# Three spacer tiles on the right side of SBUF: other byte offsets between the two operands of the matmuls

## The chip, the cores and the metric

The kernel runs on one core of a Trainium2 chip. The metric is the device time of one execution in microseconds (us). Before the change it is 840.83 us, the median of three runs (839.64 to 841.19).

## What is computed

The reference is one layer of a bidirectional encoder: 512 positions, 1024 features, float32, batch 1. In its order, with the sizes that matter:

```python
n = rms_norm(x, norm_mix_pre)                     # 512 x 1024
proj = n @ w_in                                   # 1024 x 7680: gMLP u|v, q, k, v, two gates
y_a = u * (W_s LN(gelu v) + b_s)                  # 512 x 512, chunks of 128 positions
y_b = mix over 3 groups of dilated window attention (4 heads of 128 each)   # 512 x 512
merged = sigmoid(gate_a) * (y_a @ w_branch_a) + sigmoid(gate_b) * (y_b @ w_branch_b)
h = x + rms_norm(merged @ w_out, norm_mix_post)
n2 = rms_norm(h, norm_mlp_pre)
out = h + rms_norm(relu(n2 @ w_up)**2 @ w_down, norm_mlp_post)   # w_up 1024 x 4096
```

## The kernel before, in words

**Products.** Each large product is made of three matmuls on float32r operands. An operand is split into a high part (`hi`, a rounded copy by ScalarE, L75 or L80) and a low part (`lo`, the difference, by VectorE, L76 or L81), and `mm3` (L83 to L87) adds high by high, high by low and low by high in PSUM. In `nc.tensor.matmul(ps, a, b)`, `a` is the stationary operand (128 columns, loaded by an LDWEIGHTS ahead of the matmul) and `b` is the moving one (256 or 512 columns). The trace names a matmul by its output and its two operands; PEld is the weight load, PE the matmul.

**Stages in order.** (1) `norm_x` (L152) normalises x, transposes it and writes `nh` and `nl`, which hold n with features on partitions: 8 slices of 576 columns (64 columns are repeated at the end). (2) `token_major` (L198) and the loop at L179 compute v for the three groups with a slice of n **stationary** and the weights moving (tile `pv`). In groups 1 and 2 the slice takes every fourth column of n (L218), so its four starts lie 4 bytes apart. (3) `project_qk` (L252) computes q and k of each head with `feature_tile` (L220): weights stationary, 512 columns of n **moving** (tile `pf`). Scores (`psa`, `psb`), softmax and `attend` (`py`) of the heads are placed between. (4) v and u of the gMLP branch (L460 to L477) write `yah`, `yal`; attention has written `ybh`, `ybl`. (5) The gates (n moving) and the two branch products (`yah`, `yal`, `ybh`, `ybl` moving) run through `feature_tile` at L498 and L505 and give `mh`, `ml`. (6) w_out with `mh`, `ml` stationary (tile `pd`), the two norms, and n2 into the blocks of `n2pool` (trace name `n`). (7) w_up: two tiles by `up_mm` (tile `pu`), the rest by a seven-product scheme (L676, tiles `pacc` and `ptp`) with blocks of n2 moving, 256 columns wide. (8) w_down with `hh`, `hl` stationary and the weights moving (tile `pd`); for the last four of its 32 steps the stationary tiles come out of `n2pool` (trace name `hhl`), and the weights that move are called `hl` as well.

**What sets the order.** The Tile framework orders the instructions of each engine by a simulated timeline of its own and puts semaphore waits where tiles share memory. Weights come through the SyncE queue (SP); the small loads and the rows of x for the residual come through GpSimd's (POOL): `gain` (L521) and `h2` (L576, trace name `h`) among them.

**Where the tiles lie.** Pools take memory from the left end of a partition upwards, or, with `side="right"`, from the right end downwards. On the left, the constants and small tiles end at byte 20160, and all that follows is a multiple of 256 bytes long, so nearly every left tile starts at 192 modulo 256: the split weights (`hi`, `lo`, `hl`), `mh`, `ml`, `hh`, `v0h`, `ptah`. (`perm` is 1056 bytes long, so `q1`, `q0h`, `k0h` and their like, which come after it on the left, start at 224.) The right side begins at byte 229344, which is 224 modulo 256, and its tiles are multiples of 256 bytes long too: `nl` starts at 210912, `nh` at 192480, `ybl` at 184288, `ybh` at 176096, `yal` at 167904, `yah` at 159712, and after these are released the 14 blocks of `n2pool`, from 225248 downwards. All of them start at 224 modulo 256. In this text the *difference* of a matmul is the start of the moving operand less the start of the stationary one, modulo 256 bytes:

| matmuls | moving | stationary | difference before |
|---|---|---|---|
| `pf`, n moving | right, 224 | left, 192 | 32 |
| `pf`, branch inputs moving | right, 224 | left, 192 | 32 |
| `pv`, n stationary, contiguous | left, 192 | right, 224 | 224 |
| `pv`, n stationary, every fourth column | left, 192 | right, 224 to 236 | 212 to 224 |
| `pu`, `pacc`, `ptp`, n2 moving | right, 224 | left, 192 | 32 |
| `pd` of w_out and w_down | left, 192 | left, 192 | 0 |
| `pd` with `hhl` | left, 192 | right, 224 | 224 |
| `psa`, `py` of group 0 | left | left | 0 |

Of the kernel before, what the change touches and what calls it, by code (L numbers as in the profile page):

```python
# [10 lines left out]
F32 = mybir.dt.float32  # L11
# [5 lines left out]
P = 128  # L17
# [19 lines left out]
def block_kernel(ctx: ExitStack, tc: tile.TileContext, x, norm_mix_pre, w_in, b_gate, ln_v_gain, ln_v_bias,  # L37
                 w_spatial, b_spatial, w_branch_a, w_branch_b, w_out, norm_mix_post, norm_mlp_pre, w_up,
                 w_down, norm_mlp_post, ident_c, rope_c, mask_c, perm_c, out):
    nc = tc.nc  # L40
# [3 lines left out]
    def pool(stack, name, bufs=1, space=None, side=None):  # L44
        kw = {"side": side} if side else {}
        if space is not None:
            kw["space"] = space
        return stack.enter_context(tc.tile_pool(name=name, bufs=bufs, reuse_waits="tile", **kw))
# [40 lines left out]
    def rstd_of(ss, mult, eps=EPS):  # L89
# [7 lines left out]
        nc.gpsimd.tensor_tensor(r, t, neghalf[:, :1], op=ALU.pow)  # L97
        return r

    right = ExitStack()  # L100
    npool = pool(right, "npool", side="right")
    nh = npool.tile([P, KD, S + ROT], F32R, name="nh")
# [84 lines left out]
        split_into(v0h[:, b], v0l[:, b], pv)  # L187
    start.close()

    carry = pool(right, "carry", side="right")  # L190
    ybh = carry.tile([P, NH, S], F32R, name="ybh")
    ybl = carry.tile([P, NH, S], F32R, name="ybl")
# [269 lines left out]
    for g2 in range(2):  # L462
        raw = wload([KD, 2 * P], lambda r: [(r, fcols(w_in, COL_U + g2 * 2 * P, KD, 2 * P))], "uw")
        for j in range(2):
# [8 lines left out]
            t = gpool.tile([P, 4, P], F32, name="sv", bufs=2)  # L473
# [38 lines left out]

    back = ExitStack()
    psB = pool(back, "psB", space=PSUM)
    n2pool = pool(back, "n2pool", bufs=14, side="right")
    hst = ExitStack()
    fpool = pool(hst, "fpool", side="right")
# [289 lines left out]
```

## Time and profile before

| | before |
|---|---|
| median of 3 runs | 840.83 us |
| the profiled execution | 839.99 us |
| its span, first to last instruction | 838.2 us |
| TensorE busy | 819.9 us (98%) |
| weight loads busy | 707.3 us (84%) |
| VectorE, ScalarE, GpSimd busy | 491.4, 348.6, 84.5 us |
| mean granted TensorE clock | 0.994 |
| bytes moved by DMA | 86.90 MB, mean 104 GB/s |

The page lists busy time by engine, the chain of work that ended last, and groups of instructions. Matmuls are pipelined: one that lasts 397 ns starts some 230 ns after the one before it, so the time of a stage goes by the distance from start to start (called spacing here), which the timeline shows, and not by the duration of one.

### The profile page before, as it was taken

The page shows a single profiled execution, that of the slowest core. Times are in us where ns is not written, and L with a number is a line of the kernel's source. Part 1 is how long each engine was busy: PE and PEld are TensorE (multiplying, and loading weights), DVE is VectorE, ACT ScalarE, POOL GpSimd, SP SyncE. Part 2 cuts the span into 40 slices and gives each one's busy share as a digit, 9 for nine tenths or more (in the row PEclk, how much of TensorE's full clock was granted, in tenths as well). Part 3 has the DMA queues.
Part 4 walks back from the last instruction along what each step waited for, and adds up shares of the span by engine and source line. Part 5 has one row for each costly group of instructions (what it writes and reads, how often), then busy time and mean ns, then how long its engine had stood idle before and what let it go on. Part 6 is the DMA issues. An engine that isn't in the chain of part 4 may idle for free.

```text
span 838.2 us, 10932 instructions
## 1 busy us (share of the span) xinstructions
PE 819.9 (98%) x4371; PEld 707.3 (84%) x4371; DVE 491.4 (59%) x831; ACT 348.6 (42%) x561; POOL 84.5 (10%) x78
## 2 busy tenths in 40 slices
PE   7999999999999999999999989999999999999997
PEld 5899888888888778888888879999999888888885
DVE  6422788978764737443333489989887633333324
ACT  6322243444344444323312465666666632223311
POOL 2100113223224300000000220000000100000000
PEclk9999999999999999999999989999999999999999
DMA  9432233231213233422413242334333722222202
GB/s 295 141 101 79 73 101 101 58 93 55 97 51 90 88 100 126 152 77 74 151 51 100 76 154 73 102 109 132 113 101 126 251 99 87 84 87 97 100 1 100
DMA packets 70373, 86.90 MB, mean 104 GB/s; under 512 B 2034, under 2 KB 57490, under 8 KB 70323
## 3 DMA queue, kind: packets, MB, share of 16 engines
q1 hardware_dynamic: 67810, 77.67, 29.5%
q0 software_dynamic: 2512, 8.54, 3.0%
q8 instruction: 34, 0.56, 0.3%
q14 instruction: 17, 0.13, 0.0%
HBM read 82.01 MB, written 4.19 MB: 103 GB/s over the span
## 4 chain that ended last, share of the span: by engine, by line
PE 96%; ACT 2%; DMA 1%; DVE 1%; issue 0%; SPq 0%; DVEq 0%; POOLq 0%; ACTq 0%
PE pf L87 12%; PE pf L86 12%; PE pf L85 12%; PE pacc L680 11%; PE pd L85 9%; PE pd L86 9%; PE pd L87 9%; PE ptp L680 5%; PE pv L85 4%; PE pv L87 4%; PE pv L86 4%; PE pu L85 1%; PE pu L86 1%; PE pu L87 1%; PE py L407 1%; PE psb L307 1%
## 5 line engine op out<-in xcount | busy, mean ns | idle before, releaser
L87 PE MATMUL pf<-nh,lo 128*128 128x512 f32 x352 | 139.9, 397 | 0.0
L86 PE MATMUL pf<-nl,hi 128*128 128x512 f32 x352 | 139.7, 397 | 0.0
L85 PE MATMUL pf<-nh,hi 128*128 128x512 f32 x352 | 139.5, 397 | 0.0
L680 PE MATMUL pacc<-n,hl 128*128 128x256 f32 x840 | 104.4, 279 | 0.0
L680 PEld LDWEIGHTS pacc<-n,hl 128*128 128x128 f32 x840 | 100.9, 188 | 0.2 <-ACT hl L80 0.2
L85 PE MATMUL pd<-hl,hh 128*128 128x512 f32 x224 | 87.1, 390 | 1.0 <-ACT hh L80 1.0
L86 PE MATMUL pd<-hl,hh 128*128 128x512 f32 x224 | 87.2, 389 | 0.0
L87 PE MATMUL pd<-hl 128*128 128x512 f32 x224 | 86.0, 389 | 0.0
L87 PEld LDWEIGHTS pf<-nh,lo 128*128 128x128 f32 x352 | 66.1, 188 | 15.4 <-issue 0.2
L85 PEld LDWEIGHTS pf<-nh,hi 128*128 128x128 f32 x352 | 66.1, 188 | 15.3 <-issue 0.2
L86 PEld LDWEIGHTS pf<-nl,hi 128*128 128x128 f32 x352 | 66.1, 188 | 15.2
L81 DVE TENSOR_TENSOR hl<-hid,hh 128x512 fp32r<-128x512 f32 x28 | 19.3, 693 | 80.4 <-ACT hh L80 78.9
L248 POOL TENSOR_TENSOR sw<-sw,rope 32x512 f32<-32x512 f32 x24 | 43.9, 1830 | 178.6 <-DVE sw L246 161.2
L80 ACT ACTIVATE hh<-hid 128x512 fp32r<-128x512 f32 x28 | 17.6, 631 | 93.3 <-PE pd L86 93.3
L85 PE MATMUL pv<-hi,nh 128*128 128x512 f32 x128 | 52.0, 410 | 1.1 <-ACT nh L80 1.1
L86 PE MATMUL pv<-lo,nh 128*128 128x512 f32 x128 | 51.9, 405 | 0.0
L87 PE MATMUL pv<-hi,nl 128*128 128x512 f32 x128 | 51.9, 407 | 0.0
L85 PEld LDWEIGHTS pd<-hl,hh 128*128 128x128 f32 x224 | 42.0, 188 | 10.4 <-ACT hh L80 1.4
L87 PEld LDWEIGHTS pd<-hl 128*128 128x128 f32 x224 | 42.0, 188 | 8.7
L86 PEld LDWEIGHTS pd<-hl,hh 128*128 128x128 f32 x224 | 42.0, 188 | 8.6
L97 POOL TENSOR_TENSOR rs_out<-rs_in,neghalf 128x1 f32<-128x1 f32 x20 | 14.7, 734 | 333.7 <-DVE rs_in L94 329.9
L81 DVE TENSOR_TENSOR hl<-dnw,hl 128x1024 fp32r<-128x1024 f32 x32 | 39.2, 1226 | 14.0 <-ACT hl L80 14.0
(243 smaller groups left out, 1568.0 us busy)
## 6 DMA issues: line engine op xcount, KB each, us to landing
upw<-in_w_up_dram SPq DMA_DIRECT2D x16, 1024.0 KB, 5.6
dnw<-in_w_down_dram SPq DMA_DIRECT2D x16, 1024.0 KB, 5.0
qkw<-in_w_in_dram SPq DMA_DIRECT2D x24, 512.0 KB, 4.2
gw<-in_w_in_dram SPq DMA_DIRECT2D x8, 1024.0 KB, 5.2
slab<-in_w_in_dram SPq DMA_DIRECT2D x6, 1024.0 KB, 14.0
wow<-in_w_out_dram SPq DMA_DIRECT2D x4, 1024.0 KB, 4.9
w0raw<-in_w_in_dram SPq DMA_DIRECT2D x4, 512.0 KB, 7.1
uw<-in_w_in_dram SPq DMA_DIRECT2D x2, 1024.0 KB, 5.0
```

The costliest lines, as they stand in the source:

```text
L80: nc.scalar.activation(hi, src, AF.Copy)
L81: nc.vector.tensor_tensor(lo, src, hi.bitcast(F32), op=ALU.subtract)
L85: nc.tensor.matmul(ps, ah, bh, start=start, stop=False)
L86: nc.tensor.matmul(ps, ah, bl, start=False, stop=False)
L87: nc.tensor.matmul(ps, al, bh, start=False, stop=stop)
L97: nc.gpsimd.tensor_tensor(r, t, neghalf[:, :1], op=ALU.pow)
L248: nc.gpsimd.tensor_tensor(sw, sw, rope[:, 1], op=ALU.mult)
L307: nc.tensor.matmul(ps[:, rr, g - 1], got["q", g][:, r], got["k", g][:, r], start=True, stop=True)
L407: nc.tensor.matmul(o, v12[:, g, r, hs], ptb[r // 2][:, r % 2, g], start=False, stop=(r == 3 and g == 1), skip_group_check=True)
L680: nc.tensor.matmul(ps, a[:, j], b[:, j], start=first and not (j or m), stop=(j == KH - 1 and m == 2), skip_group_check=True)
```

## The change

A function `spacer` allocates a tile on the right side and has GpSimd set it to zero. It is called three times, so that the right side begins 32 bytes lower from the start, the branch inputs lie another 160 bytes lower, and n2 and all that shares its side lie 224 bytes lower than after the first spacer alone.

```diff
+    def spacer(stack, nbytes, name):
+        t = pool(stack, name, side="right").tile([P, nbytes // 4], F32, name=name)
+        nc.gpsimd.memset(t, 0.0)
+
+    spacer(ctx, 32, "edge")
     right = ExitStack()
     npool = pool(right, "npool", side="right")
...
     start.close()
 
+    spacer(right, 160, "yedge")
     carry = pool(right, "carry", side="right")
...
     psB = pool(back, "psB", space=PSUM)
+    spacer(back, 224, "nedge")
     n2pool = pool(back, "n2pool", bufs=14, side="right")
```

The starts modulo 256 become 192 for `nh` and `nl`, 32 for `ybh`, `ybl`, `yah` and `yal`, and 224 again for the blocks of `n2pool`.

## The prediction

> **What bounds the kernel now.** I read the page first: busy time by engine, the chain that ended last, and the costliest groups.
>
> ```profile
> span 838.2 us, 10932 instructions
> PE 819.9 (98%) x4371; PEld 707.3 (84%) x4371; DVE 491.4 (59%) x831; ACT 348.6 (42%) x561; POOL 84.5 (10%) x78
> ...
> PE 96%; ACT 2%; DMA 1%; DVE 1%; issue 0%; SPq 0%; DVEq 0%; POOLq 0%; ACTq 0%
> ...
> L87 PE MATMUL pf<-nh,lo 128*128 128x512 f32 x352 | 139.9, 397 | 0.0
> L86 PE MATMUL pf<-nl,hi 128*128 128x512 f32 x352 | 139.7, 397 | 0.0
> L85 PE MATMUL pf<-nh,hi 128*128 128x512 f32 x352 | 139.5, 397 | 0.0
> ...
> L85 PE MATMUL pv<-hi,nh 128*128 128x512 f32 x128 | 52.0, 410 | 1.1 <-ACT nh L80 1.1
> ```
>
> TensorE is busy 98% of the span, and 96% of the chain is its own matmuls. Whatever shortens the distance between two matmul starts shortens the kernel, as long as the other engines keep up. The largest consumer is `pf` with n moving: 3 x 352 = 1056 matmuls of 512 columns. With n stationary there are 3 x 128 = 384 more.
>
> Second, the stages one by one (columns: PE, PEld, DVE, ACT and POOL busy, granted clock, DMA share, GB/s):
>
> ```profile
> 39.00:84.00 45.00, 45.00 (x191) 44.91 (x191) 11.51 (x12) 10.24 (x13) 0.00 (x0) 1.00 0.31 85
> 84.00:172.00 88.00, 88.00 (x426) 72.65 (x425) 72.11 (x149) 35.03 (x72) 21.59 (x13) 1.00 0.33 89
> 172.00:269.00 97.00, 97.00 (x505) 81.50 (x504) 70.50 (x184) 40.52 (x82) 28.33 (x16) 1.00 0.21 66
> 340.00:440.00 100.00, 100.00 (x430) 80.33 (x429) 35.52 (x44) 28.47 (x38) 0.00 (x0) 1.00 0.29 96
> ```
>
> In every stage that works with n, PE has no gap and the clock is full; VectorE, the next busiest, is at 72.11 of 88 us in the worst one. So these stages are paced by the matmul stream itself, weight loads running beside it.
>
> Third, does that stream run at one speed? All 512-column matmuls do the same work; the tile views give their durations (ns, minimum/median/maximum).
>
> ```profile
> L85 PE MATMUL pd<-hl,hh x224: 387/389/498, 650.0 to 808.9; 128*128 128x512 f32 x112
> ...
> L85 PE MATMUL pd<-hi,mh x64: 389/389/398, 439.9 to 483.7; 128*128 128x512 f32 x64
> ...
> L85 PE MATMUL pd<-hl,hhl x32: 392/395/396, 809.5 to 831.2; 128*128 128x512 f32 x32
> ```
>
> ```profile
> L85 PE MATMUL pf<-nh,hi x352: 388/396/483, 83.6 to 433.6; 128*128 128x512 f32 x176
> ...
> L85 PE MATMUL pf<-ybh,hi x32: 390/395/505, 314.6 to 436.4; 128*128 128x512 f32 x32
> ...
> L85 PE MATMUL pf<-yah,hi x32: 393/396/477, 319.4 to 439.2; 128*128 128x512 f32 x32
> ```
>
> They fall in two classes, 389 ns and 395 to 396 ns, and the classes follow the table of differences above: 0 modulo 256 for `hh` and `mh`; 32 for `nh`, `ybh` and `yah`; 224 for `hhl`. The last pair says most: `hh` and `hhl` are the same w_down matmul, on the same weights, and only the place of the stationary tile changes. The spacing, from the timeline (first and last start of a run of equal matmuls):
>
> ```profile
> 360.09 0.40 PE L85 MATMUL pf<-nh,hi 128*128 128x512 f32 x1
> ...
> 363.59 0.39 PE L85 MATMUL pf<-nh,hi 128*128 128x512 f32 x1
> ...
> 700.05 0.39 PE L85 MATMUL pd<-hl,hh 128*128 128x512 f32 x1
> ...
> 703.45 0.39 PE L85 MATMUL pd<-hl,hh 128*128 128x512 f32 x1
> ...
> 822.13 0.40 PE L85 MATMUL pd<-hl,hhl 128*128 128x512 f32 x1
> ...
> 824.93 0.40 PE L85 MATMUL pd<-hl,hhl 128*128 128x512 f32 x1
> ```
>
> 15 matmuls of `pf` take 3.50 us, 233.3 ns each. 15 of `pd` with `hh` take 3.40 us, 226.7 ns. 12 with `hhl` take 2.80 us, 233.3 ns. So difference 0 is worth 6.6 ns per matmul of 512 columns against 32 and 224.
>
> **The change part by part.** *n moving (`pf`): 32 becomes 0.* 1056 x 6.6 ns = 7.0 us, all on the path, since PE has no gap in these stages. What is late next is VectorE; 72.11 us of work in a stage shortened from 88 to about 86 us still leaves it slack, so I give nothing back.
>
> *n stationary, contiguous (`pv` of group 0 and of the gMLP): 224 becomes 0.* 192 matmuls x 6.6 ns = 1.3 us.
>
> *n stationary, every fourth column (`pv` of groups 1 and 2): 212 to 224 become 244 to 256.* Also 192 matmuls. No row shows these differences.
>
> ```profile
> 70.09 0.40 PE L85 MATMUL pv<-hi,nh 128*128 128x512 f32 x1
> ...
> 74.38 0.40 PE L85 MATMUL pv<-hi,nh 128*128 128x512 f32 x1
> ```
>
> 18 matmuls in 4.29 us are 238.3 ns each. PEld is busy 44.91 of 45 us here, so the strided weight load may be a limit of its own. Ends: nothing, or the full 6.6 ns (1.3 us); a loss is bounded by the step from 233.3 to 238.3, the worst against the usual, 5.0 x 192 = 1.0 us. I take 0.6 us of gain, half of the full step, because only one of the four slices comes to exactly 0.
>
> *Branch inputs moving: 32 becomes 96.* 2 x 3 x 32 = 192 matmuls. Difference 96 does not occur before. Of the differences that do occur at this width, only 0 is fast; 32 and 224 both give 233.3 ns, and 96 lies between these two. I take no change. Ends: 192 x 6.6 = 1.3 us of gain, 1.0 us of loss by the step above.
>
> *n2 and `hhl`: 32 + 224 = 256 lower, so no difference changes.* Nothing. That part only undoes the first spacer for them.
>
> *The three memsets.* GpSimd runs them.
>
> ```profile
> 0.74 0.10 POOL L60 MEMSET neghalf<- 128x2 f32 x1 [0.29 <-POOLq L796]
> ...
> 321.35 0.61 POOL L521 DMA_DIRECT2D gain<-in_norm_mix_post_dram  x1 [38.88 <-DVE yal L81]
> 325.02 0.54 POOL L576 DMA_DIRECT2D h<-in_x_dram  x1 [3.06 <-ACT hi L75]
> 326.84 0.54 POOL L576 DMA_DIRECT2D h<-in_x_dram  x1 [1.28 <-DVE yal L81]
> 468.36 0.56 POOL L97 TENSOR_TENSOR rs_out<-rs_in,neghalf 128x1 f32<-128x1 f32 x1 [140.98 <-DVE rs_in L94]
> ```
>
> A memset of this size lasts about 0.1 us. `edge` and `yedge` lie on memory that nobody used before and wait for nothing. `nedge` lies where the end of `nl` was, so it waits for the last matmul that reads `nl`. If it stands ahead of `gain` and the two loads of `h` in GpSimd's queue, these three, now issued at 321 to 327 us, wait with it. Who needs them, and when `nl` is free:
>
> ```profile
> 433.83 0.40 PE L86 MATMUL pf<-nl,hi 128*128 128x512 f32 x1
> ```
>
> ```profile
> 465.33 0.69 DVE L545 TENSOR_TENSOR y<-pd,gain 128x512 f32<-128x512 f32 x1 [15.54 <-ACT n2f L541]
> ```
>
> ```profile
> gain<-in_norm_mix_post_dram POOLq DMA_DIRECT2D x1, 512.0 KB, 4.2
> ```
>
> Issued at about 434.5, `gain` lands some 4 to 5 us later, 25 us before its first reader at 465.33. I cost it at nothing; the w_out stage hides it, and without that cover it would be the 5 us of issue and landing.
>
> *Sum:* 7.0 + 1.3 + 0.6 = 8.9 us. Against the profiled execution (839.99 us, of which 838.2 is the span) that is 831.1 us. That execution is 0.8 us below the median of the runs, 840.83, and 840.83 - 8.9 = 831.9 gives the forecast, 832.0 us.
>
> **The rivals.** *1. It is not the offset.* All 512-column rows at difference 0 have both operands on the left side; all others cross the sides. Were the side the cause, nothing would move: 840.8 us. Against it: `hh` lies at bytes 126656 to 134848 and `hhl` from 172000 on, so a border would have to fall just between. The Trainium skill speaks for this rival and against the change: in "TensorE: Matmul & The Clock Gate", section "Step-by-step: what each phase is for", moving and stationary operands have read ports of their own, and loading the next weights takes nothing from the running matmul. By that rule no offset could matter and the time would stay at 840.8 us; the 389 against 395 ns of `hh` and `hhl` disagree with it. Chance 0.08.
>
> *2. Difference 0 is the worse one, and the time rises.* The matmuls of 256 columns say so:
>
> ```profile
> 129.63 0.28 PE L87 MATMUL psa<-k0h,q0l 128*128 128x256 f32 x1
> ...
> 130.59 0.28 PE L87 MATMUL psa<-k0h,q0l 128*128 128x256 f32 x1
> ...
> 603.10 4.83 PE L680 MATMUL pacc<-n,hl 128*128 128x256 f32 x40
> 607.77 1.33 PE L680 MATMUL ptp<-n,hl 128*128 128x256 f32 x10
> ```
>
> At difference 0 (`psa`) 8 matmuls take 0.96 us, 120 ns each; at 32 (`pacc`) 40 take 4.67 us, 116.8 ns. If each load of weights costs those 3.2 ns more with n at 0, then 1056 + 384 matmuls cost 4.6 us and the time is 845.4 us. It decides once the spacing of `pf` in the new trace exceeds 233.3 ns. Against it: the 512-column rows measure width 512 itself. Chance 0.05.
>
> *3. The gain is had, but part is lost to the clock.*
>
> ```profile
> 490.30:497.10 6.80, 6.25 (x27) 5.96 (x28) 4.20 (x7) 4.77 (x8) 3.14 (x1) 0.50 0.59 187
> ```
>
> After the waits ahead of w_up the clock is granted at half for 6.8 us; 6.25 us of matmuls would take half of that at full clock, so the spell costs 3.1 us. The stage comes some 8 us earlier after the change, and a spell may be added or drop out: 835.1 or 828.9 us. The Trainium skill's section "Part 1: The HAM clock gate (the "warmup" mystery)" on the same page has the clock judged in free-running windows of about 3.4 us; the 6.8 us here agree with two of them, and by that rule where they fall differs from execution to execution. Chance that a further spell moves it upwards by that much: 0.15.
>
> **How the numbers follow.** The forecast has 0.72, rivals 3, 1 and 2 have 0.15, 0.08 and 0.05. A measurement of this kernel can tell about 0.2% (1.7 us) from no change. Forecast and rival 3 both lie faster by more: 0.87. Rival 1 is no change, 0.08; rival 2 is slower, 0.05. The range: downwards the forecast less a dropped spell, 828.9, rounded to 829.0; upwards rival 3 with the losses of 1.0 us each for the strided and the branch matmuls, 837.1, rounded to 837.0. That leaves out rivals 1 and 2 and a little of the rest.
>
> **What would show it.** Right: median duration of `pf` with n 389 ns instead of 396, spacing 226.7 ns, the stage of the gates and q, k shorter by 3%; `pacc`, `pd` and `hhl` as before; `pv` with contiguous n at 389; `gain` landed well before its first reader. Wrong: `pf` stays at 395 to 396 (rival 1) or rises over it (rival 2); VectorE or the weight splits appear as what PE waits for in the stages of n; `yah` and `ybh` above 396; a second stretch at half clock.

## The result, and the profile after

The changed kernel takes 832.73 us (median of 6 runs, 832.43 to 834.43), against 840.18 us (839.31 to 841.19, 6 runs) for the kernel before on the same chip. The ratio is 0.9914, with a 95% interval of 0.9901 to 0.9927: 7.45 us or 0.9% faster. The forecast was 832.0 us, in a range of 829.0 to 837.0.

First the page of the changed kernel: span, busy time, chain, and the groups of `pf` with n.

```profile
span 830.7 us, 10935 instructions
PE 812.6 (98%) x4371; PEld 706.5 (85%) x4371; DVE 491.6 (59%) x831; ACT 348.6 (42%) x561; POOL 83.0 (10%) x81
...
PE 96%; ACT 2%; DMA 1%; DVE 1%; issue 0%; SPq 0%; DVEq 0%; POOLq 0%; ACTq 0%
...
L87 PE MATMUL pf<-nh,lo 128*128 128x512 f32 x352 | 138.2, 393 | 0.0
L86 PE MATMUL pf<-nl,hi 128*128 128x512 f32 x352 | 138.1, 392 | 0.0
L85 PE MATMUL pf<-nh,hi 128*128 128x512 f32 x352 | 137.8, 392 | 0.0
```

The span is 7.5 us shorter, and TensorE's busy time fell by 7.3 us with the same number of matmuls. Nothing else on the first two lines moved by more than 1.5 us, and GpSimd has its three memsets more (81 against 78). The mean of a `pf` row with n went from 397 to 392 or 393 ns, so not all the way to the 389 of w_down. The tile views of the changed kernel, minimum/median/maximum in ns:

```profile
L85 PE MATMUL pf<-nh,hi x352: 387/389/481, 82.5 to 426.6; 128*128 128x512 f32 x176
...
L85 PE MATMUL pf<-ybh,hi x32: 392/397/494, 309.4 to 429.4; 128*128 128x512 f32 x32
...
L87 PE MATMUL pf<-yah,lo x32: 394/399/399, 320.9 to 432.6; 128*128 128x512 f32 x32
```

The median of n is 389, as forecast; the mean stays above it because of a tail. The branch inputs stand a little over the 395 to 396 of before. In the timeline both parts of n's distribution can be seen:

```profile
383.26 0.40 PE L85 MATMUL pf<-nh,hi 128*128 128x512 f32 x1
383.50 0.40 PE L86 MATMUL pf<-nl,hi 128*128 128x512 f32 x1
383.73 0.39 PE L87 MATMUL pf<-nh,lo 128*128 128x512 f32 x1
383.96 0.39 PE L85 MATMUL pf<-nh,hi 128*128 128x512 f32 x1
384.19 0.40 PE L86 MATMUL pf<-nl,hi 128*128 128x512 f32 x1
384.42 0.39 PE L87 MATMUL pf<-nh,lo 128*128 128x512 f32 x1
384.65 0.40 PE L85 MATMUL pf<-nh,hi 128*128 128x512 f32 x1
...
390.10 0.39 PE L85 MATMUL pf<-nh,hi 128*128 128x512 f32 x1
...
393.50 0.39 PE L85 MATMUL pf<-nh,hi 128*128 128x512 f32 x1
```

383.26 us is the first matmul with n after a product with the branch inputs. The next six starts come at 232 ns on average (1.39 us); later, from 390.10 to 393.50, 15 matmuls take 3.40 us, 226.7 ns each. After an interruption the stream settles at the fast spacing only some matmuls later: after about eight here, after two to ten elsewhere in this trace. Counted over all 1056 matmuls of n in the trace: 830 are followed by the next start within 228 ns (mean 226.7), 203 after 229 to 260 ns (mean 232.9), and 23 after more, where another product or a wait lies between. Before the change the counts were 12, 1021 (mean 233.3) and 23.

GpSimd's part, from the timeline of the changed kernel:

```profile
0.77 0.10 POOL L102 MEMSET edge<- 128x8 f32 x1
0.81 0.13 POOL L102 MEMSET yedge<- 128x40 f32 x1
...
316.16 0.61 POOL L528 DMA_DIRECT2D gain<-in_norm_mix_post_dram  x1 [38.18 <-DVE yal L81]
319.83 0.54 POOL L583 DMA_DIRECT2D h<-in_x_dram  x1 [3.06 <-ACT hi L75]
...
427.25 0.14 POOL L102 MEMSET nedge<- 128x56 f32 x1 [105.00 <-PE pf L86]
```

`nedge` did wait for the last reader of `nl`, but the planner put it behind the three loads, so nobody waits for it. The clock was granted at half for 6.8 us ahead of w_up once more, as before:

```profile
483.00:489.80 6.80, 6.02 (x26) 5.73 (x27) 4.30 (x8) 4.77 (x8) 3.14 (x1) 0.50 0.51 173
```

### The profile page after: what moved, and what is told of

Its sections match the earlier page's. It is cut to its first block, busy times and chain, and to the rows that moved or that the text cites. A ratio compares the mean times of both kernels' runs of the same rounds, so it can differ in the third digit from the quotient of the medians.

```text
span 830.7 us, 10935 instructions
## 1 busy us (share of the span) xinstructions
PE 812.6 (98%) x4371; PEld 706.5 (85%) x4371; DVE 491.6 (59%) x831; ACT 348.6 (42%) x561; POOL 83.0 (10%) x81
## 4 chain that ended last, share of the span: by engine, by line
PE 96%; ACT 2%; DMA 1%; DVE 1%; issue 0%; SPq 0%; DVEq 0%; POOLq 0%; ACTq 0%
PE pf L87 12%; PE pf L86 11%; PE pf L85 11%; PE pacc L687 11%; PE pd L85 9%; PE pd L87 9%; PE pd L86 9%; PE ptp L687 5%; PE pv L85 4%; PE pv L86 4%; PE pv L87 4%; PE pu L85 1%; PE pu L87 1%; PE pu L86 1%; PE py L413 1%; PE psb L313 1%
## 5 line engine op out<-in xcount | busy, mean ns | idle before, releaser
L87 PE MATMUL pf<-nh,lo 128*128 128x512 f32 x352 | 138.2, 393 | 0.0
L85 PE MATMUL pf<-nh,hi 128*128 128x512 f32 x352 | 137.8, 392 | 0.0
L254 POOL TENSOR_TENSOR sw<-sw,rope 32x512 f32<-32x512 f32 x24 | 42.2, 1760 | 175.1 <-DVE sw L252 158.0
L75 ACT ACTIVATE hi<-qkw 128x1024 fp32r<-128x1024 f32 x24 | 25.4, 1058 | 49.3 <-PE pf L86 25.5
```

The source lines that it names most:

```text
L75: nc.scalar.activation(hi, raw, AF.Copy)
L85: nc.tensor.matmul(ps, ah, bh, start=start, stop=False)
L87: nc.tensor.matmul(ps, al, bh, start=False, stop=stop)
L254: nc.gpsimd.tensor_tensor(sw, sw, rope[:, 1], op=ALU.mult)
```

## The experiments

Two theories were to be told apart. The **offset theory**: the spacing of matmuls goes by the difference between the starts of the moving and the stationary operand modulo 256 bytes. The **side theory**: matmuls whose operands lie on different sides of SBUF are slow, wherever they start. Kernels that were timed ran against the kernel before on the same chip; each ratio below is to that.

**1. A sweep over the differences.** The edit, in place of the whole computation:

```python
for w in (512, 256):
    for o in range(65):                  # moving rows start 4*o bytes further on
        for i in range(48):
            nc.tensor.matmul(acc[:, :w], st[:, i % 8], mv[:, o:o + w], start=i == 0, stop=i == 47)
```

> This kernel leaves the whole computation out: it copies x to the output and runs nothing but streams of 48 matmuls on the left side of SBUF, with the start of the moving rows moved on by 4 bytes from stream to stream (65 starts, 0 to 256 bytes from the start of the stationary tiles), at 512 and at 256 columns; no other engine works meanwhile. Offset theory (the spacing goes by the difference of the two starts modulo 256 bytes): at 512 columns 226.7 ns at 0 and 256, 233.3 at 32 and 224; at 256 columns more at 0 (120 ns) than at 32 (117). Side theory (only operands on different sides are slow): one spacing throughout, 226.7 ns. Open: what 96 gives, and whether any difference beats 0.

The timeline merges equal matmuls; from each stream a stretch with its start, length and count (the length holds the whole of the last matmul, 0.39 or 0.28 us, which comes off):

```profile
726.71 9.00 PE L59 MATMUL acc<-mv,st 128*128 128x512 f32 x39
...
100.83 9.03 PE L59 MATMUL acc<-mv,st 128*128 128x512 f32 x38
...
278.76 9.03 PE L59 MATMUL acc<-mv,st 128*128 128x512 f32 x38
...
736.57 5.44 PE L59 MATMUL acc<-mv,st 128*128 128x256 f32 x44
...
781.93 5.30 PE L59 MATMUL acc<-mv,st 128*128 128x256 f32 x44
...
1011.34 4.94 PE L59 MATMUL acc<-mv,st 128*128 128x256 f32 x42
```

The first is difference 256, which is 0: 8.61 us over 38 steps, 226.6 ns. The second is 32 and the third 96: 8.64 over 37, 233.5 ns each. At 256 columns, 0 gives 5.16 over 43, 120.0 ns; 32 gives 116.7; 192 gives 4.66 over 41, 113.7, with four matmuls at the start that are not yet settled. All tiles lie on the left side here, so the side theory falls. Means over the settled part of each stream, from the starts of the matmuls, in ns:

| difference (bytes) | 0 | 4 | 16 | 20 | 28 | 32 | 64 | 96 | 128 | 132 | 160 | 192 | 224 |
|---|---|---|---|---|---|---|---|---|---|---|---|---|---|
| 512 columns | 226.7 | 236.6 | 231.7 | 240.0 | 226.6 | 233.4 | 228.9 | 233.3 | 233.5 | 240.0 | 234.3 | 233.2 | 233.4 |
| 256 columns | 120.0 | 123.4 | 113.4 | 122.2 | 115.5 | 116.7 | 117.8 | 119.9 | 118.7 | 122.4 | 118.6 | 113.3 | 118.4 |

At 512 columns nothing was faster than 226.7, and 0 is among several that reach it. At 256 columns 0, at 120.0, is slower than 32 and 192, which is why both signs stood in the trace of before.

**2. Only the first spacer.**

```diff
-    spacer(right, 160, "yedge")
-    spacer(back, 224, "nedge")
```

> The first spacer alone: n, the branch inputs, the blocks of n2 and hhl all come to difference 0. Offset theory: n gains as in the changed kernel (7.5 us); branch inputs gain 192 x 6.6 = 1.3 us and hhl 96 x 6.6 = 0.6 us on the kernel before; n2 at 0 costs (120 - 116.8) x 1368 = 4.4 us if the rows of 256 columns in the trace of before hold. Sum 840.2 - 9.4 + 4.4 = 835.2 us; 830.8 us if n2 does not mind. Side theory: 840.2 us, no change.

834.28 us, ratio 0.9933 (0.9915 to 0.9951). The rows of `pacc`, at difference 32 in the kernel before and at 0 here, from the tile views:

```profile
L680 PE MATMUL pacc<-n,hl x840: 276/280/384, 517.4 to 659.6; 128*128 128x256 f32 x168
...
L685 PE MATMUL pacc<-n,hl x840: 278/283/387, 509.4 to 655.1; 128*128 128x256 f32 x168
```

The median went from 280 to 283 ns and the mean spacing of `pacc` and `ptp` (distances under 150 ns) from 116.9 to 120.0; n, the branch inputs and `hhl` ran at 389. So the offset theory holds on both counts, and the third spacer, which takes n2 back to 32, is worth about 3 us: the 1368 matmuls of n2 cost 166.7 us here against 163.6 in the changed kernel. A second spell at half clock fell into this execution:

```profile
309.60:313.00 3.40, 3.40 (x8) 2.71 (x9) 3.40 (x6) 1.46 (x3) 0.00 (x0) 0.50 0.03 5
```

It costs about 1.7 us (half of 3.40), and it is rival 3 of the prediction seen in another kernel. The profiled executions of the control (experiment 8) and of n2 at 192 in the kernel before (experiment 6) have such a spell of 3.4 us too, at 314 us; those of before and after have none there.

**3. The spacer on the left side instead**, in the kernel before:

```diff
+    lsp = pool(ctx, "ledge").tile([P, 8], F32, name="ledge")
+    nc.gpsimd.memset(lsp, 0.0)
     wstack = ExitStack()
```

> The kernel before with a spacer of 32 bytes on the left side instead, ahead of the weights: all left tiles start at 224 modulo 256 as the right ones do, so every difference is that of the run with the first spacer alone, while the starts themselves are 32 modulo 64. Offset theory: the same time as that run (835 us or 831 us). Theory of the starts themselves (a tile that starts at 32 modulo 64 is slow): n gains nothing and the matmuls of w_out and w_down lose 864 x 6.6 = 5.7 us, 845.9 us. Side theory: 840.2 us.

833.7 us, ratio 0.9928 (0.9910 to 0.9945): the same as experiment 2, and between the two times that were expected, with the tiles of both sides at 224 modulo 256.

```profile
L87 PE MATMUL pf<-nh,hi x352: 387/389/479, 83.4 to 426.0; 128*128 128x512 f32 x176
...
L682 PE MATMUL pacc<-n,hl x840: 278/283/384, 509.2 to 654.9; 128*128 128x256 f32 x168
```

n gains the same, n2 loses the same. Whether the tiles start at 192 or at 224 does not matter; what counts is the difference.

**4. A difference of 224 between two tiles on the left.** In the changed kernel:

```diff
+    dsp = pool(dn, "dsp").tile([P, 8], F32, name="dsp")
+    nc.gpsimd.memset(dsp, 0.0)
     dpool = pool(dn, "dpool", bufs=2)
```

> The changed kernel with a spacer of 32 bytes ahead of the pool of the stationary tiles of w_down, so that 648 of its matmuls go from difference 0 to 224 with both operands still on the left side. Offset theory: 648 x 6.6 = 4.3 us more than the changed kernel, 837.0 us, median duration of these rows 395 to 396 ns. Side theory: no change, 832.7 us and 389 ns.

836.88 us, ratio 0.9967 (0.9956 to 0.9979), that is some 4 us over the changed kernel. The tile view:

```profile
L85 PE MATMUL pd<-hl,hh x224: 389/396/502, 643.8 to 806.9; 128*128 128x512 f32 x112
...
L85 PE MATMUL pd<-hi,mh x64: 389/389/397, 434.0 to 477.8; 128*128 128x512 f32 x64
```

The shifted rows of w_down went from 389 to 396 ns without leaving their side, while w_out, which was not touched, stayed at 389. Summed from start to start, w_down took 158.2 us in place of 153.9: the 4.3 us that were expected. The prediction could not tell side from offset; this run does.

**5. Without the second spacer.** The edit is the first line of experiment 2 alone.

> The changed kernel without its second spacer: the branch inputs come to difference 0 in place of 96, n stays at 0 and n2 at 32. Offset theory, with the sweep's 233.4 ns at 96 and 226.7 at 0: 192 matmuls save 1.3 us or a little more, 831.4 us, and their median duration falls to 389 ns. If a stream of branch matmuls stood to gain from 96, it would be above 832.7 us.

830.12 us, ratio 0.9899 (0.9883 to 0.9915). Run once more, beside the changed kernel:

> The changed kernel once more, beside the one without the second spacer on the same chip: 832.7 us.

> The changed kernel without the second spacer, beside the changed kernel on the same chip. Offset theory: 192 x 6.7 = 1.3 us to 192 x 9 = 1.7 us below it, 831.2 us.

833.31 us, ratio 0.9915 (0.9898 to 0.9933), and 830.63 us, ratio 0.9886 (0.9873 to 0.9899). Its tile view:

```profile
L85 PE MATMUL pf<-ybh,hi x32: 387/389/496, 308.4 to 426.9; 128*128 128x512 f32 x32
```

The branch inputs run at 389 in place of 397, and the 192 matmuls cost 44.0 us in place of 45.3. The second spacer thus costs 1.3 us directly. The medians lie 2.7 us apart on the same chip, and the intervals of the two ratios just overlap, so that the rest of the gap is not shown to be the spacer's. The two profiled executions, 834.47 and 830.46 us, speak against it: n2, at 32 in both, took 164.6 and 163.6 us, and contiguous v, at 0 in both, 47.4 and 46.5. No kernel here was faster than this one; that of experiment 6 equals it within the intervals.

**6. n2 at 192**, which the sweep puts at 113.3 ns. Added to experiment 5 by making the third spacer 64 bytes:

```diff
-    spacer(right, 160, "yedge")
-    spacer(back, 224, "nedge")
+    spacer(back, 64, "nedge")
```

> The differences that the sweep points to and the 32-byte steps of the allocator allow: n and the branch inputs at 0, the blocks of n2 at 192 (113.3 ns in the sweep at 256 columns against 116.7 at 32), which brings hhl to 64 (228.9 ns). Offset theory: against the changed kernel 192 x 6.7 = 1.3 us, 1368 x 3.4 = 4.6 us and 96 x 4.4 = 0.4 us less, 826.4 us. If the sweep does not carry over to a kernel in which other engines work, 831 to 833 us.

830.87 us, ratio 0.9898 (0.9885 to 0.9911): no better than experiment 5. The w_up stage in its timeline:

```profile
593.33 4.87 PE L686 MATMUL pacc<-n,hl 128*128 128x256 f32 x40
598.04 1.34 PE L686 MATMUL ptp<-n,hl 128*128 128x256 f32 x10
```

From the first `pacc` to the first `ptp` 40 matmuls take 4.71 us, 117.8 ns each, where the sweep had 113.3. `hhl`, at 64, did run at 228.9. But the same execution has the fast spacing as well, earlier in the stage, up to a wait for split weights:

```profile
519.67 2.88 PE L686 MATMUL pacc<-n,hl 128*128 128x256 f32 x24
...
531.23 0.74 PE L686 MATMUL pacc<-n,hl 128*128 128x256 f32 x4 [0.52 <-ACT hl L80]
```

24 matmuls, 23 steps in 2.60 us, are 113.0 ns. In the trace 121 matmuls in a row, from 516.7 to 530.4 us, go at 113.3 ns; after the waits around 531 us the stage starts again at 117.8 and keeps it for its last 965. These 965 x 4.5 ns are 4.3 us, nearly all of what is missing to the 826.4 us that were expected. The same offset of n2 alone, in the kernel before (one spacer of 96 bytes ahead of `n2pool`):

> The kernel before with one spacer of 96 bytes ahead of the blocks of n2: n and the branch inputs stay at 32, n2 goes to 192 and hhl to 64. Offset theory: 4.6 + 0.4 us less than before, 834 to 835 us, with 113.3 ns from start to start in the stage of w_up. Otherwise no change from before.

839.53 us, ratio 0.9984 (0.9969 to 1.0000). But its twelve times fall in two groups: five from 834.95 to 836.45, and seven from 839.39 to 840.88, at the same mean clocks of 0.993 and 0.994. The lower group is where 113.3 ns would put it. The profiled execution is one of the upper group; it too has 121 matmuls at 113.3 ns, a wait, and then 964 at 117.8. At 113.3 these would take 4.3 us less, which is also the distance between the medians of the two groups (835.55 and 839.87). The spell at half clock in this execution is worth 1.7 us at most and can't make that gap. That the two groups are these two spacings is still argued, since no profile of the lower group was taken.

**7. The sweep with the kernel's structure, idle and busy.**

```python
for g in range(4):                       # one of four streams: the order of the seven-product scheme
    for j in range(4):
        for m, (a, b) in enumerate(((sth, mvh), (sth, mvl), (stl, mvh))):
            nc.tensor.matmul(accs[g % 3][:, :256], a[:, 2 * j], b[:, 256 * j + o:256 * j + o + 256], ...)
```

> Like the first sweep it leaves the computation out and runs only matmuls on an otherwise idle core, for 16 differences in steps of 16 bytes. Four streams at each: 512 columns with a matmul of 128 columns after every 24; 256 columns plain; 256 columns in groups of 12 that go to three PSUM banks in turn; and 256 columns in the kernel's own order of operands (high by high, high by low, low by high, in groups of 12). The question: the w_up stage ran at 117.7 ns at difference 192 where the first sweep had 113.3. If the order of operands or the groups are the reason, the last two streams show 117 to 118 ns at 192 and the plain one 113.3. If the stream alone decides, all show 113.3, and the other engines of the kernel are left as the reason. The 512-column stream should need some ten matmuls at 231 to 236 ns after each interruption before it settles at 226.7 at difference 0.

> The same streams while ScalarE copies and VectorE subtracts 1024 columns in SBUF the whole time. If the accesses of other engines disturb the two streams of TensorE, 192 at 256 columns goes from 113.3 to 117 ns or more, and the spacings spread. If TensorE's reads are apart from theirs, both sweeps give the same numbers.

The two sweeps gave the same settled spacings to 0.1 ns at all 16 differences, although in the second ScalarE and VectorE were busy throughout:

```profile
100.00:200.00 100.00, 100.00 (x664) 91.54 (x663) 97.28 (x80) 97.11 (x92) 0.00 (x0) 1.00 0.00 1
```

Plain, in groups, and in the kernel's order, 256 columns took 120.0 ns at 0, 116.7 at 32 and 113.3 at 192. So neither the work of ScalarE and VectorE nor the order or the banks explain the 117.8 of experiment 6. (DMA and GpSimd stood still in these sweeps; the two spacings within one execution, above, say that the work around the stream is not needed as a reason.) At 512 columns an interruption at difference 32 changed nothing for long, since that stream is at 233 ns anyway. At 0 the stream was back at 226 to 227 ns from the second matmul after the last interruption on, so the ten slow matmuls that I expected there did not come. They did come earlier in that stream, when it passed from the 427 ns of its first matmuls to full speed: ten at 224 to 236 ns, then 226.7. So an interruption can be followed by such a stretch, but need not be. At difference 240 this sweep settled at 233.3 ns where the first had 226.7.

**8. A control.** The kernel before with `spacer(ctx, 256, "edge")` alone.

> A control: the kernel before with one spacer of 256 bytes at the right end, so that every right tile moves and GpSimd has a memset more, while no difference changes. Offset theory: the time of the kernel before, within 0.2%, and 395 to 396 ns for n. If what helped were the place in memory, the order of the instructions or the memsets, it would come near 832 us.

839.46 us, ratio 0.9997 (0.9988 to 1.0005), with n where it was:

```profile
L85 PE MATMUL pf<-nh,hi x352: 388/396/483, 83.4 to 434.6; 128*128 128x512 f32 x176
```

Moving all right tiles by 256 bytes, and a memset more, make no difference that these runs can tell.

## Why the prediction was right, point by point

Summed from the traces: the distances from each matmul start to the next, by what the matmul reads, in us (a distance over 2 us counts as 2).

| matmuls | before | after | no second spacer | first spacer alone |
|---|---|---|---|---|
| n moving, 1056 | 248.5 | 243.0 | 242.7 | 242.7 |
| n stationary, contiguous, 192 | 48.0 | 47.2 | 46.5 | 47.6 |
| n stationary, every fourth column, 192 | 45.6 | 45.1 | 45.1 | 45.1 |
| branch inputs moving, 192 | 45.2 | 45.3 | 44.0 | 45.3, in a half-clock spell |
| n2 moving, 1368 | 163.9 | 163.6 | 163.6 | 166.7 |
| `hhl` | 22.2 | 22.2 | 22.2 | 21.5 |
| w_out and w_down, 864 | 199.5 | 199.4 | 199.4 | 199.4 |

From before to after these rows fall by 7.1 us in all; the profiled executions lie 7.5 us apart (839.99 and 832.47), and the matmuls outside the table make up the rest. The sum of the prediction was 8.9 us.

- *n moving, 7.0 us.* Right in kind, too large: 5.5 us. The full 6.6 ns were charged to all 1056 matmuls; 830 of them got it, 830 x 6.6 = 5.5 us. The spacing of 226.7 ns belongs to a settled stream, and after most interruptions by transposes, scores or the branch products two to ten matmuls come at some 232 ns on average before it settles. The steady rows that I quoted could not show that, because w_down has hardly any interruption. This is the mis-sized term. The rows of n became 2.2% shorter, where 3% was named as the sign.
- *n stationary, contiguous, 1.3 us.* 0.8 us in the table, of which 0.4 us is clear: the 96 matmuls of the gMLP took 22.7 us before and 22.3 after, with the median duration at 389 as forecast. They lose the rest to interruptions too, by the attention of the last head. The 96 of group 0 took 25.3 and 24.9 us, but that half says little: the first matmuls of the kernel start 427 ns apart, 12 of them before and 11 after, and their number moves this row more than the offset does. Without the second spacer they were 7, which gives the 46.5 us of that column.
- *n stationary, every fourth column, 0.6 us.* 0.5 us. That half of a full step was right is luck rather than reasoning. The reason given was that only one slice of four comes to exactly 0, but that slice is no faster than the others. In the trace after, the spacing alternates between 231 and 238 to 240 ns from each matmul to the next, also where nine in a row read the same slice:

```profile
69.10 0.39 PE L85 MATMUL pv<-hi,nh 128*128 128x512 f32 x1
69.33 0.40 PE L86 MATMUL pv<-lo,nh 128*128 128x512 f32 x1
69.57 0.40 PE L87 MATMUL pv<-hi,nl 128*128 128x512 f32 x1
69.80 0.40 PE L85 MATMUL pv<-hi,nh 128*128 128x512 f32 x1
70.04 0.39 PE L86 MATMUL pv<-lo,nh 128*128 128x512 f32 x1
```

By slice, in the order of the program, the means are 235.6 ns at difference 0, and 233.9, 235.9 and 234.4 at 252, 248 and 244. The sweep, with contiguous weights, has 226.7, 226.7, 230.0 and 240.0 there, so its figures do not carry over to strided weight loads.
- *Branch inputs, no change.* 0.1 us slower, inside the ends given. The sweep's 233.3 ns at 96 agrees with the guess; it was still a loss against 0, which experiment 5 took. Their median durations, 397 and 399 ns, are over the 396 that the prediction named as a sign of being wrong; the sign came, but it was worth 0.1 us.
- *n2 and `hhl`, no change.* Right (0.3 us and 0.0). What I called merely undoing the first spacer is the part that keeps about 3 us (experiment 2).
- *The memsets, nothing.* Right; the price would have been nothing even without the cover that I named, since the order put the loads first.
- *Rival 1* (no effect): experiments 1, 3, 4 and 8 rule it out. The rule of the Trainium skill on which it leaned, in "TensorE: Matmul & The Clock Gate", section "Step-by-step: what each phase is for", is that loading the next weights takes no read bandwidth from the running matmul. The measurement decides: in experiment 1 the relative place of the two operands alone makes 226.7 or 240.0 ns.
- *Rival 2* (0 is worse) is true at 256 columns, 120.0 against 116.7 ns, and false at 512. Between 0 and 32 the width decides the sign, so the evidence of one width says nothing of the other.
- *Rival 3* (the clock): the spell of 6.8 us stayed as it was in the changed kernel, and no further one came. In three of the other profiled executions one did, of 3.4 us (experiment 2), so the chance given to it was not idle.

Open: what makes the differences fast or slow inside the chip, and what decides, when a stream starts again after a wait, whether it goes on at 113.3 or at 117.8 ns at 256 columns and difference 192.

## What to carry to other kernels

Where a kernel is a dense stream of weight loads and matmuls, compare the spacing of equal matmuls across stages. If it differs with nothing else to tell them apart, look at where the moving and the stationary tiles start relative to each other, and try a spacer of 32 to 224 bytes before anything larger. Take the best difference for each width from a sweep of the real shapes, and time it in the kernel, since a stream can settle in more than one pattern.

## What was not expected of the hardware

- The spacing depends on the difference down to 4 bytes: at 512 columns 226.7 ns at 0, 236.6 at 4, 240.0 at 20 and at 132.
- A stream keeps a pattern once it has settled, and the same difference can settle in two: 226.7 or 233.3 ns at 240 bytes and 512 columns (two sweeps), 113.3 or 117.8 ns at 192 bytes and 256 columns (one execution, before and after a wait).
- ScalarE and VectorE at 97% busy on SBUF did not move a single one of the settled spacings of experiment 7 by more than 0.1 ns.
- A weight load that takes every fourth column lasts 308 to 311 ns in place of 188 in the changed kernel, yet its matmuls start every 235 ns, whichever slice they read.
